# A Hyena and latent-attention encoder layer: the implicit filter on 128 rows of half the times, constant tables in two parts over GpSimd's queue

## Chip, cores and metric

The kernel runs on one core of a Trainium2 chip. The metric is the device time of one execution in microseconds (us); lower is better. The cores' engines are TensorE (PE, with its weight loads as PEld), VectorE (DVE), ScalarE (ACT), GpSimd (POOL) and SyncE (SP), which here only issues DMAs. Each engine works off its own list of instructions in order, and each DMA queue belongs to the engine that issues on it.

## The reference

One layer on x of 1024 x 1024 in float32: a root-mean-square norm, one input projection of 5,280 columns, a Hyena branch with two gated long convolutions, a branch of latent attention with eight heads, gates, and an output projection. The change touches the implicit filter of the long convolutions:

```python
def hyena_filter_spectra(L, w_f1, b_f1, freq_1, w_f2, b_f2, freq_2, w_f3):
    ...
    z = jnp.concatenate([t, jnp.cos(ang), -jnp.sin(ang)], axis=-1)
    h = jnp.sin(freq_1 * (z @ w_f1 + b_f1))
    h = jnp.sin(freq_2 * (h @ w_f2 + b_f2))
    k = (h @ w_f3).reshape(L, HY_ORDER, 2, HY_WIDTH)
    ...
    k = k * decay[:, None, None, :]
    k_full = jnp.concatenate([k[:, :, 0], k[::-1, :, 1]], axis=0)
    return jnp.fft.rfft(k_full.astype(jnp.float32), axis=0)
```

L is 1024, z has 33 columns, h has 64, HY_WIDTH is 512. The filter has two directions, and the second runs through time backwards.

## The kernel before, in words

Products of float32 are made from parts: a value is split into a high part (a cast to the PE's fp32r type, on ScalarE) and a low part (the difference, on VectorE), by `split` and `gsplit`. `mm3` makes a product from three matmuls: high by high, low by high, high by low. So each operand costs a ScalarE cast and a VectorE subtraction before TensorE can use it.

The work around the change comes in this order.

- `load_x` loads x as eight tiles of 128 x 1024, by SyncE's and ScalarE's queues in turn.
- `filter_loads` issues on SyncE's queue the constant selection matrix (`selr`), the two hidden weights, and the network's input table `z2` of 128 x 1024: rows 0 to 32 hold z, rows 64 to 96 hold z with reversed time. So the 128 rows carry both directions of the filter, and all 1024 times stand in the columns.
- `build_hT` makes the normalised, transposed x. It takes the sums of squares on both engines, then a reciprocal root of twelve small VectorE operations (`rsqrt`), scales x (`xs`, L223), transposes it on TensorE (`ptx`, L230), and splits what it gets from PSUM (`hh` on ScalarE, L142; `hl` on VectorE, L143). It does so for two halves of the times, of four x tiles each.
- `filter_mlp` is the two hidden layers. Each goes in two groups of 512 times: three matmuls into one PSUM bank (`pf`), then `sin_layer` with six VectorE steps over 128 x 512 (bias and frequency L254, turns L255 and L256, three reductions L258 and a clamp L260) and the sine on ScalarE (L261), whose table must be loaded when another function ran before (ACT_TABLE_LOAD). The first layer's output is split into `h1h` and `h1l`; of the second's, `h` holds for each direction the high part on its 64 rows, and the residual on the other 64 (L305, L306).
- `filter_tables` loads the last layer's weights by ScalarE's queue, puts their high part on both row halves with four casts of 64 x 1024 (`w3h`, L319), the low part on one and zeros on the other (`w3l`, L322), and splits the forward transform's table `ku` (`kuh`, `kul`).
- `filter_spectra` multiplies `h` by `w3h` and `w3l` (`pk`, L348 and L349, 128 x 256 each), applies the decay (`kk`), and transforms the filters (`forward`, `pu`).
- `fill_g` are blocks of the input projection (`proj_block`): 48 matmuls of 128 x 512 each (`pm`, L567) on weights of 128 x 4 x 128 (`wr`, L559, two buffers on SyncE's queue; `wh`, `wl` their parts, L138, L139). They need nothing of the filter. The scheduler of the tile framework sets them between the filter's instructions on TensorE, so that they fill its waits. It fixes each engine's order when the program is built. An eviction `ob` (L683) ends a block.
- `load_gu` loads and splits the tables of the later transforms (`gu`) while the convolutions are under way.

## Time and profile before

| | |
|---|---|
| runs, us | 1154.97, 1155.45, 1157.68; median 1155.45 |
| profiled execution | 1159.08 us, span 1156.9 us |
| mean granted TensorE clock | 0.984 of full speed |
| busy share of the span | PE 95%, PEld 79%, DVE 77%, ACT 51%, POOL 9% |
| chain that ended last | PE 77%, DVE 8%, DMA 8%, ACT 4%, issue 2%, POOL 1% |

The profile is of one execution. A busy time is the sum over an engine's instructions; the share is of the span. The chain that ended last is followed back from the last instruction, at each step to what released it. In the timelines a number in brackets is the engine's idle time ahead of the instruction, with what ended it. A matmul's time includes its way through the array, so matmuls overlap: what one costs in a row of many is the distance of their starts.

### The profile page before, as it was taken

The numbers are of one execution on the slowest core, as the hardware profiler recorded it, in microseconds if no ns is written. First come the engines' busy times: TensorE is split into PE (matmuls) and PEld (weight loads), VectorE is DVE, ScalarE is ACT, GpSimd is POOL, SyncE is SP. The second block draws the span as 40 slices with busy tenths as digits, with TensorE's granted clock in tenths as the row PEclk, the third lists the DMA queues.
The fourth block names the chain that finished last, engine by engine and source line by source line (L and its number), as shares of the span: only waits on it lengthen the run. The fifth ranks groups of instructions, "written<-read, shape, count | busy, mean of one in ns | idle before, by whom it ended". The sixth has DMA issues, their size and how long they took to land.

```text
span 1156.9 us, 15518 instructions
## 1 busy us (share of the span) xinstructions
PE 1098.8 (95%) x5525; PEld 912.7 (79%) x5525; DVE 894.0 (77%) x1631; ACT 589.2 (51%) x1097; POOL 106.7 (9%) x108
## 2 busy tenths in 40 slices
PE   4899999999999999999998999799999999999996
PEld 3678888888888888878887887688888888777875
DVE  6988788698788886778774793488888888678872
ACT  5735655754445434434424752687777777321420
POOL 0000000000000000000000132400000000232253
PEclk9989999999999999999999999899999999999999
DMA  5446454642335334334327558610202010886345
GB/s 211 132 146 194 153 166 175 204 119 64 88 90 142 110 110 131 91 90 125 91 82 226 153 152 284 201 56 12 90 1 92 1 65 1 265 272 208 90 129 182
DMA packets 119221, 150.27 MB, mean 130 GB/s; under 512 B 8548, under 2 KB 82408, under 8 KB 119144
## 3 DMA queue, kind: packets, MB, share of 16 engines
q1 hardware_dynamic: 107688, 120.97, 34.4%
q10 hardware_dynamic: 11456, 28.32, 6.5%
q8 instruction: 43, 0.70, 0.3%
q14 instruction: 34, 0.28, 0.1%
HBM read 101.81 MB, written 47.45 MB: 129 GB/s over the span
## 4 chain that ended last, share of the span: by engine, by line
PE 77%; DVE 8%; DMA 8%; ACT 4%; issue 2%; POOL 1%; SPq 0%; POOLq 0%; ACTq 0%; DVEq 0%
PE pm L567 35%; PE pu L128 8%; PE pt L901 5%; PE pi L128 4%; PE S L119 2%; PE S L121 2%; PE S L122 2%; PE pv L913 2%; PE pv L914 2%; PE po L122 2%; PE po L121 2%; PE po L119 2%; PE pmo L121 1%; PE pmo L119 1%; ACT pr L888 1%
## 5 line engine op out<-in xcount | busy, mean ns | idle before, releaser
L567 PE MATMUL pm<-hh,wh 128*128 128x512 f32 x656 | 208.8, 394 | 1.4 <-DVE hl L143 0.5
L567 PE MATMUL pm<-hl,wh 128*128 128x512 f32 x656 | 209.4, 394 | 0.0
L567 PE MATMUL pm<-hh,wl 128*128 128x512 f32 x656 | 208.3, 392 | 0.1
L567 PEld LDWEIGHTS pm<-hh,wh 128*128 128x128 f32 x656 | 123.1, 189 | 27.3 <-ACT wh L138 0.7
L567 PEld LDWEIGHTS pm<-hh,wl 128*128 128x128 f32 x656 | 123.4, 189 | 26.0 <-DVE wl L139 0.5
L567 PEld LDWEIGHTS pm<-hl,wh 128*128 128x128 f32 x656 | 123.5, 189 | 25.4
L138 ACT CAST wh<-wr 128x512 fp32r<-128x512 f32 x98 | 60.3, 621 | 152.0 <-PE pm L567 106.9
L138 ACT CAST PTh<-pt 128x512 fp32r<-128x512 f32 x128 | 72.8, 587 | 43.6 <-PE pt L901 41.8
L139 DVE TENSOR_TENSOR PTl<-pt,PTh 128x512 fp32r<-128x512 f32 x128 | 84.0, 683 | 14.0 <-ACT PTh L138 13.7
L886 DVE TENSOR_REDUCE mx<-S 128x1 f32<-128x1024 f32 x64 | 77.8, 1218 | 10.5 <-PE S L122 10.1
L139 DVE TENSOR_TENSOR wl<-wr,wh 128x512 fp32r<-128x512 f32 x95 | 66.2, 702 | 16.2 <-ACT wh L138 16.1
L901 PE MATMUL pt<-ident,pr 128*128 128x128 f32 x512 | 75.1, 276 | 1.1 <-ACT pr L888 0.2
L888 ACT ACTIVATE pr<-S,mx 128x1024 f32<-128x1024 f32 x64 | 71.7, 1121 | 5.4 <-DVE mx L886 5.1
L901 PEld LDWEIGHTS pt<-ident,pr 128*128 128x128 f32 x512 | 59.1, 140 | 15.5 <-ACT pr L888 2.9
L913 PE MATMUL pv<-PTh,vc 128*128 128x256 f32 x256 | 68.9, 297 | 0.0
L914 PE MATMUL pv<-PTl,vc 128*128 128x256 f32 x256 | 67.8, 293 | 0.0
L473 DVE TENSOR_TENSOR t<-pu,kt 128x512 f32<-128x512 f32 x64 | 41.0, 681 | 31.2 <-PE pu L128 30.5
L138 ACT CAST rh<-res 128x512 fp32r<-128x512 f32 x64 | 39.5, 619 | 42.8 <-PE pu L128 20.2
L119 PE MATMUL S<-kh,qh 96*128 96x512 f32 x128 | 53.0, 414 | 1.7 <-ACT pr L888 1.6
L121 PE MATMUL S<-kh,ql 96*128 96x512 f32 x128 | 52.5, 410 | 0.0
L913 PEld LDWEIGHTS pv<-PTh,vc 128*128 128x128 f32 x256 | 48.5, 189 | 4.4 <-DVE at L924 1.6
L122 PE MATMUL S<-kl,qh 96*128 96x512 f32 x128 | 50.8, 398 | 0.0
(285 smaller groups left out, 2402.2 us busy)
## 6 DMA issues: line engine op xcount, KB each, us to landing
wr<-in_w_in_dram SPq DMA_DIRECT2D x82, 256.0 KB, 3.2
wor<-in_w_out_dram SPq DMA_DIRECT2D x36, 256.0 KB, 4.6
dec<-in_dec_dram SPq DMA_DIRECT2D x16, 512.0 KB, 3.7
gT<-ob ACTq DMA_DIRECT2D x16, 512.0 KB, 3.3
gg<-gT SPq DMA_DIRECT2D x16, 512.0 KB, 3.9
kd<-kt ACTq DMA_DIRECT2D x28, 256.0 KB, 2.2
kt<-kd SPq DMA_DIRECT2D x28, 256.0 KB, 2.7
m<-gg ACTq DMA_DIRECT2D x16, 256.0 KB, 3.5
```

Source lines behind the costliest of these rows:

```text
L119: m = nc.tensor.matmul(out, lhsT=lh, rhs=rh, start=start, stop=False)
L121: nc.tensor.matmul(out, lhsT=ll, rhs=rh, start=False, stop=False)
L122: nc.tensor.matmul(out, lhsT=lh, rhs=rl, start=False, stop=stop)
L128: m = self.nc.tensor.matmul(out, lhsT=x, rhs=y, start=n == 0, stop=n == len(ops) - 1)
L138: self.behind(self.nc.scalar.copy(out=hi, in_=x), after)
L139: (eng or self.nc.vector).tensor_tensor(out=lo, in0=x, in1=hi.bitcast(F32), op=ALU.subtract)
L567: nc.tensor.matmul(ps[c][0:m], lhsT=w[:, i, 0:m], rhs=h[d][:, c * 512:(c + 1) * 512], start=(d == 0 and f == 0), stop=(d == 7 and f == 2))
L886: nc.vector.tensor_reduce(out=mx, in_=ps, axis=AX.X, op=ALU.max, negate=True)
L888: nc.scalar.activation(out=pr, in_=ps, func=AF.Exp, bias=mx, accum_out=RS[h // 2][:, qb, h % 2:h % 2 + 1])
L901: nc.tensor.transpose(out=pt[:, i], in_=pr[:, kb * P:(kb + 1) * P], identity=self.ident)
L913: nc.tensor.matmul(pv, lhsT=V[h][:, kb], rhs=hi[:, kb], start=(kb == 0), stop=False)
L914: nc.tensor.matmul(pv, lhsT=V[h][:, kb], rhs=lo[:, kb], start=False, stop=(kb == 7))
```

## The change

The input table holds half as many columns: rows 0 to 32 carry the first 512 times, rows 64 to 96 the last 512. Each hidden layer is then one group of three matmuls and one `sin_layer`. That has two reductions in place of three, and one buffer of each kind. The filter of reversed times is no longer computed: a VectorE copy reads `h` with reversed columns. Since both directions now need all 128 rows of the last layer's weights, these are loaded on both row halves by four loads on SyncE's queue, and split like any other operand, in 128 x 1024.

The tables `z2`, `ku` and `gu` are split on the host, and `sel` is passed as fp32r. GpSimd's queue loads all of them straight into their places: the first five behind a copy that waits for the seventh x tile, `guh` and `gul` later. The splits of these tables on ScalarE and VectorE go. Ahead of the real transposes stand 36 of raw x whose result nobody reads.

```diff
-    z2 = np.zeros((P, L), f32)
-    z2[:33] = z.T
-    z2[64:97] = z[::-1].T
+    z2 = np.zeros((P, L // 2), f32)
+    z2[:33] = z[:L // 2].T
+    z2[64:97] = z[L // 2:].T
...
+    for n, x in (("z2", z2), ("ku", ku), ("gu", gu)):
+        t[n + "h"], t[n + "l"] = _parts(x)
...
+        idle = self.pp.tile([P, 512], F32, tag="tp", bufs=2, name="idle")
+        for i in range(4):
+            for j in range(8 if i < 3 else 12):
+                nc.tensor.transpose(out=idle[:, :P], in_=xt[i][:, (j % 8) * P:(j % 8 + 1) * P], identity=self.ident)
...
-        for c in (6.28125, 0.0019350051879882812, 3.019915981956753e-07):
+        for c in (6.28125, 2 * math.pi - 6.28125):
...
-        self.selr = f1.tile([P, P], F32, tag="selr", name="selr")
-        nc.sync.dma_start(out=self.selr, in_=a["sel"])
...
-        self.z2 = f1.tile([P, L], F32, tag="z2", name="z2")
-        nc.sync.dma_start(out=self.z2, in_=a["z2"])
+        self.wf3 = [f1.tile([P, 2, HY], F32, tag=f"wf3{d}", name=f"wf3{d}") for d in range(2)]
+        w3v = a["w_f3"][0].rearrange("k (o d c) -> d k o c", o=2, d=2)
+        for d in range(2):
+            for s in range(2):
+                nc.sync.dma_start(out=self.wf3[d][64 * s:64 * s + 64], in_=w3v[d])
+
+        dum = f1.tile([1, 1], F32, tag="dum", name="xdum")
+        last = nc.gpsimd.tensor_copy(out=dum, in_=self.xt[6][0:1, 0:1])
...
+        for t, x in ((self.z2[0], "z2h"), (self.z2[1], "z2l"), (self.kuh, "kuh"), (self.kul, "kul"), (self.sel, "sel")):
+            i = nc.gpsimd.dma_start(out=t, in_=a[x])
+            self.behind(i, last)
+            last = i
...
+        ps = self.pp.tile([P, L // 2], F32, tag="cv", bufs=CVB, name=self.nm("pf"))
+        self.mm3(ps, w1h, w1l, zh, zl, True, True)
+        x = self.sin_layer(f1, ps, fv[:, 0:1], fv[:, 1:2], L // 2)
+        self.split(x, h1h, h1l)
+        for d in range(2):
+            self.split(self.wf3[d], self.w3h[d], self.w3l[d], after=self.half0)
+        ps = self.pp.tile([P, L // 2], F32, tag="cv", bufs=CVB, name=self.nm("pf"))
+        self.mm3(ps, w2h, w2l, h1h, h1l, True, True)
+        x = self.sin_layer(f1, ps, fv[:, 2:3], fv[:, 3:4], L // 2)
         for c in range(2):
...
+            a_, b_ = slice(64 * c, 64 * c + 64), slice(64 - 64 * c, 128 - 64 * c)
+            h, r = self.h2[0, c], self.h2[1, 1 - c]
+            nc.scalar.copy(out=h[a_], in_=x[a_])
+            nc.vector.tensor_tensor(out=h[b_], in0=x[a_], in1=h[a_].bitcast(F32), op=ALU.subtract)
+            nc.vector.tensor_copy(out=r, in_=h[:, ::-1].bitcast(F32))
...
-        for i in range(2):
-            r = self.uq.tile([P, 11, P], F32, tag="UY", bufs=2, name=self.nm("gur"))
-            nc.sync.dma_start(out=r, in_=self.a["gu"][:, 11 * i:11 * i + 11])
-            self.split(r, self.guh[:, 11 * i:11 * i + 11], self.gul[:, 11 * i:11 * i + 11])
+        for t, x in ((self.guh, "guh"), (self.gul, "gul")):
+            nc.gpsimd.dma_start(out=t, in_=self.a[x])
```

The change moves instructions at three places that matter below; each list is one engine's own order.

On TensorE, ahead of the first spectrum product `pk` (`pm` with number 1630 and 1631 is the projection block that fills the wait; all `pm` rows here are of that block). Before:

```order
L567 MATMUL pm_1630<-hl_154,wh_1664 128x512
L567 MATMUL pm_1631<-hl_154,wh_1664 128x512
L567 MATMUL pm_1630<-hh_146,wl_1665 128x512
L567 MATMUL pm_1631<-hh_146,wl_1665 128x512
L348 MATMUL pk_475<-w3h_340,h_344 128x256
L349 MATMUL pk_475<-w3l_342,h_344 128x256
L348 MATMUL pk_475<-w3h_340,h_344 128x256
L349 MATMUL pk_475<-w3l_342,h_344 128x256
L348 MATMUL pk_481<-w3h_341,h_345 128x256
```

Now (the block that 1630 and 1631 were has the numbers 1617 and 1618; 1683 and 1684 are the next block; h_397 is a reversed copy):

```order
L569 MATMUL pm_1683<-hh_158,wh_1717 128x512
L569 MATMUL pm_1684<-hh_158,wh_1717 128x512
L569 MATMUL pm_1683<-hl_166,wh_1717 128x512
L350 MATMUL pk_462<-w3h_391,h_395 128x256
L351 MATMUL pk_462<-w3l_393,h_395 128x256
L350 MATMUL pk_462<-w3h_391,h_395 128x256
L351 MATMUL pk_462<-w3l_393,h_395 128x256
L569 MATMUL pm_1684<-hl_166,wh_1717 128x512
L569 MATMUL pm_1683<-hh_158,wl_1718 128x512
L569 MATMUL pm_1684<-hh_158,wl_1718 128x512
L350 MATMUL pk_468<-w3h_392,h_397 128x256
```

Before, the first `pk` stood right behind the end of the block. Now 33 matmuls of the next block stand between that end and `pk`: 53 instructions lie from the second layer's first matmul (`pf_428`) to `pk`, of which the twentieth is the last of block 1617 and 1618. Between the first layer's matmuls and the second's lie 43, and three more `pm` stand between the first `pk` and that on the reversed copy.

On ScalarE, around the two sines (`sx`). Before:

```order
L683 ACTIVATE ob_1692<-pm_1630,cols 128x512
L261 ACT_TABLE_LOAD
L261 ACTIVATE sx_398<-sx_398 128x512
L261 ACTIVATE sx_416<-sx_416 128x512
L305 CAST h_344<-sx_398 64x512
L305 CAST h_345<-sx_398 64x512
L305 CAST h_344<-sx_416 64x512
L305 CAST h_345<-sx_416 64x512
L683 ACT_TABLE_LOAD
L683 ACTIVATE ob_1692<-pm_1631,cols 128x512
```

Now:

```order
L147 CAST wh_1687<-wr_1685 128x512
L271 ACT_TABLE_LOAD
L271 ACTIVATE sx_413<-sx_413 128x512
L147 CAST wh_1717<-wr_1715 128x512
L147 CAST h1h<-sx_413 128x512
L147 CAST wh_1753<-wr_1751 128x512
L147 CAST wh_1783<-wr_1781 128x512
L683 ACT_TABLE_LOAD
L683 ACTIVATE ob_1679<-pm_1617,cols 128x512
L271 ACT_TABLE_LOAD
L271 ACTIVATE sx_432<-sx_432 128x512
L683 ACT_TABLE_LOAD
```

Behind the last of these rows stand the second half's eviction, `ob_1679<-pm_1618`, and then the casts h_395 and h_396. The first layer's sine (`sx_413`) and the cast of its output (`h1h`) stand behind and between casts of projection weights, and the second's (`sx_432`) behind an eviction of the block, with a table load on either side.

On SyncE's queue, behind the last x load. Before:

```order
L267 DMA selr<-in_sel_dram 128x128
L269 DMA wf_133<-in_wf_dram 128x128
L271 DMA wf_135<-in_wf_dram 128x128
L273 DMA z_137<-in_z_dram 128x1024
L559 DMA wr_1566<-in_w_in_dram 128x4x128
L559 DMA wr_1596<-in_w_in_dram 128x4x128
```

Now:

```order
L277 DMA wf_131<-in_wf_dram 128x128
L279 DMA wf_133<-in_wf_dram 128x128
L285 DMA wf_135<-in_w_f_dram 64x2x512 x2
L285 DMA wf_136<-in_w_f_dram 64x2x512 x2
L561 DMA wr_1553<-in_w_in_dram 128x4x128
L561 DMA wr_1583<-in_w_in_dram 128x4x128
```

Four loads of the last layer's weights (`w_f`) have come ahead of the first projection weights, and the selection matrix and the input table have left.

## Rows read from the trace of the kernel before

**Rows 1.** The page's part 1: busy us of each engine, share of span, instructions.

```profile
PE 1098.8 (95%) x5525; PEld 912.7 (79%) x5525; DVE 894.0 (77%) x1631; ACT 589.2 (51%) x1097; POOL 106.7 (9%) x108
```

**Rows 2.** Waits of PE over the whole span: us in total, times, longest us.

```profile
PE pk L348 <- DVE h L306: 5.9, 1, 5.9
...
PE pq L119 <- ACT q L794: 1.8, 1, 1.8
```

**Rows 3.** Windows, columns: PE, PEld, DVE, ACT, POOL busy (x), PEclk, DMA share, GB/s.

```profile
60.00:65.00 5.00, 4.55 (x14) 3.58 (x14) 4.07 (x7) 2.18 (x4) 0.00 (x0) 0.50 0.55 170
```

**Rows 4.** Timeline of PE, 45 to 67 us: start, us, line, form, [idle before].

```profile
45.67 0.61 PE L567 MATMUL pm<-hl,wh 128*128 128x512 f32 x2
...
49.02 0.62 PE L567 MATMUL pm<-hh,wh 128*128 128x512 f32 x2
...
51.77 0.62 PE L567 MATMUL pm<-hh,wh 128*128 128x512 f32 x2
...
52.68 0.61 PE L567 MATMUL pm<-hh,wl 128*128 128x512 f32 x2
59.19 0.58 PE L348 MATMUL pk<-w3h,h 128*128 128x256 f32 x1 [5.90 <-DVE h L306]
...
66.07 0.63 PE L567 MATMUL pm<-hh,wl 128*128 128x512 f32 x2
```

**Rows 5.** Groups of DVE, 25 to 60 us: busy us, mean ns, idle before.

```profile
L258 DVE SCALAR_TENSOR_TENSOR sx<-sk,sx 128x512 f32<-128x512 f32 x12 | 7.6, 688 | 0.0
L254 DVE TENSOR_SCALAR sx<-pf,cols 128x512 f32<-128x512 f32 x4 | 3.1, 807 | 0.1
...
L322 DVE TENSOR_TENSOR w3l<-wf,w3h 64x1024 fp32r<-64x1024 f32 x2 | 2.4, 1218 | 0.0
...
L256 DVE TENSOR_SCALAR sk<-sk 128x512 f32<-128x512 f32 x4 | 1.6, 422 | 0.0
```

**Rows 6.** Groups of ACT, 25 to 70 us.

```profile
L319 ACT CAST w3h<-wf 64x1024 fp32r<-64x1024 f32 x4 | 4.2, 1049 | 3.1 <-DMA wf<-in_w_f_dram 3.0
L683 ACT ACT_TABLE_LOAD x3 | 3.8, 1283 | 0.1
...
L683 ACT ACTIVATE ob<-pm,cols 128x512 f32<-128x512 f32 x4 | 2.8, 688 | 1.9 <-PE pm L567 1.9
...
L138 ACT CAST zh<-z 128x512 fp32r<-128x512 f32 x2 | 1.1, 620 | 0.0
```

**Rows 7.** Weight loads: the page's part 6; then the first eight's landing alone.

```profile
wr<-in_w_in_dram SPq DMA_DIRECT2D x82, 256.0 KB, 3.2
...
DMA to landing us min/median/max: 3.0/4.3/5.1
```

**Rows 8.** Timeline of the start, 15 to 31 us.

```profile
15.95 6.01 PE L230 MATMUL ptx<-ident,xs 128*128 128x128 f32 x28 [8.63 <-DVE xs L223]
...
17.75 0.62 ACT L138 CAST wh<-wr 128x512 fp32r<-128x512 f32 x1 [0.18 <-DMA wr<-in_w_in_dram]
...
20.92 0.17 DVE L158 SCALAR_TENSOR_TENSOR ry<-rt,ry 128x4 f32<-128x4 f32 x1
...
22.47 0.50 PE L567 MATMUL pm<-hh,wh 128*128 128x512 f32 x1 [0.51 <-DVE hl L143]
...
22.80 0.40 PE L567 MATMUL pm<-hl,wh 128*128 128x512 f32 x1
...
28.98 1.47 PE L230 MATMUL ptx<-ident,xs 128*128 128x128 f32 x12
```

**Rows 9.** Windows of the start, columns as in rows 3.

```profile
5.00:10.00 5.00, 0.45 (x1) 0.18 (x1) 0.86 (x1) 2.43 (x3) 0.00 (x0) 1.00 1.03 417
```

**Rows 10.** A window where the gate tables are split, columns as in rows 3.

```profile
210.00:240.00 30.00, 29.84 (x147) 24.79 (x146) 19.99 (x31) 20.39 (x35) 0.26 (x4) 1.00 0.64 189
```

**Rows 11.** A window in the attention's projections, columns as in rows 3.

```profile
660.00:690.00 30.00, 28.24 (x133) 25.20 (x132) 29.07 (x99) 20.06 (x41) 10.47 (x9) 0.94 0.53 159
```

**Rows 12.** Timeline of DVE at the first filter layer.

```profile
36.57 0.81 DVE L254 TENSOR_SCALAR sx<-pf,cols 128x512 f32<-128x512 f32 x1
```

More of the change, by code (lines that the diff above doesn't have):

```diff
@@ L39, with _parts, near @@
     _r += _c
+def _parts(x):
+    def near(v):
+        u = np.ascontiguousarray(v, np.float32).view(np.uint32)
+        return ((u + 0x7FF + ((u >> 12) & 1)) & np.uint32(0xFFFFF000)).view(np.float32)
+    hi = near(x)
+    return hi, near(x - hi)
 def _constants():
@@ L187, in columns @@
         self.ssc = cp.tile([P, 2, 8], F32, tag="ssc", name="ssc")
-    def selection(self):
-        self.sel = self.cp.tile([P, P], F32R, tag="sel", name="sel")
-        self.nc.scalar.copy(out=self.sel, in_=self.selr)
     def load_x(self, xp, g):
@@ L250, in sin_layer @@
         n = cols
-        x = fp.tile([P, n], F32, tag="sx", bufs=2, name=self.nm("sx"))
-        k = fp.tile([P, n], F32, tag="sk", bufs=2, name=self.nm("sk"))
+        x = fp.tile([P, n], F32, tag="sx", name=self.nm("sx"))
+        k = fp.tile([P, n], F32, tag="sk", name=self.nm("sk"))
         mg = 12582912.0
@@ L298, in filter_mlp @@
-        for c in range(2):
-            sl = slice(c * 512, (c + 1) * 512)
-            ps = self.pp.tile([P, 512], F32, tag="cv", bufs=CVB, name=self.nm("pf"))
-            self.mm3(ps, w2h, w2l, h1h[:, sl], h1l[:, sl], True, True)
-            x = self.sin_layer(f1, ps, fv[:, 2:3], fv[:, 3:4], 512)
-            for d in range(2):
-                a_, b_ = slice(64 * d, 64 * d + 64), slice(64 - 64 * d, 128 - 64 * d)
-                nc.scalar.copy(out=self.h2[d][a_, sl], in_=x[a_])
-                nc.vector.tensor_tensor(out=self.h2[d][b_, sl], in0=x[a_], in1=self.h2[d][a_, sl].bitcast(F32), op=ALU.subtract)
@@ L308, in filter_tables @@
-    def filter_tables(self, fp):
-        nc, a = self.nc, self.a
-        self.kuh = fp.tile([P, 18, P], F32R, tag="kuh", name="kuh")
-        self.kul = fp.tile([P, 18, P], F32R, tag="kul", name="kul")
-        with self.pool("fp2") as f2:
-            wf3 = f2.tile([P, 2, HY], F32, tag="wf3", name="wf3")
-            w3v = a["w_f3"][0].rearrange("k (o d c) -> d k o c", o=2, d=2)
-            for d in range(2):
-                nc.scalar.dma_start(out=wf3[64 * d:64 * d + 64], in_=w3v[d])
-            for d in range(2):
-                for s in (slice(0, 64), slice(64, 128)):
-                    nc.scalar.copy(out=self.w3h[d][s], in_=wf3[64 * d:64 * d + 64])
-                s = slice(64 * d, 64 * d + 64)
-                nc.gpsimd.memset(self.w3l[d][64 - 64 * d:128 - 64 * d].bitcast(F32), 0.0)
-                nc.vector.tensor_tensor(out=self.w3l[d][s], in0=wf3[s], in1=self.w3h[d][s].bitcast(F32), op=ALU.subtract)
-            for i in range(2):
-                kur = f2.tile([P, 9, P], F32, tag="kur", bufs=2, name=self.nm("kur"))
-                nc.scalar.dma_start(out=kur, in_=a["ku"][:, 9 * i:9 * i + 9])
-                self.split(kur, self.kuh[:, 9 * i:9 * i + 9], self.kul[:, 9 * i:9 * i + 9])
@@ L346, in filter_spectra @@
                         for i in range(2):
-                            ts = slice((2 * tp + i) * P, (2 * tp + i + 1) * P)
-                            nc.tensor.matmul(ps[:, i], lhsT=h2[d][:, ts], rhs=w3h[d][:, o, cs], start=True, stop=False)
-                            nc.tensor.matmul(ps[:, i], lhsT=h2[d][:, ts], rhs=w3l[d][:, o, cs], start=False, stop=True)
+                            b = 2 * tp + i
+                            h = h2[d, b // 4][:, b % 4 * P:(b % 4 + 1) * P]
+                            nc.tensor.matmul(ps[:, i], lhsT=h, rhs=w3h[d][:, o, cs], start=True, stop=False)
+                            nc.tensor.matmul(ps[:, i], lhsT=h, rhs=w3l[d][:, o, cs], start=False, stop=True)
                         nc.vector.tensor_tensor(out=kk[:, d], in0=ps, in1=dec[:, d], op=ALU.mult)
@@ L1167, in hyena_mla_kernel @@
                     k.load_x(xp, 1)
-                    k.filter_loads(f1)
+                    k.filter_loads(fp, f1)
                     k.build_hT(hp, xp)
                     k.filter_mlp(fp, f1)
-                    k.selection()
                 svw = ExitStack()
                 k.vw = svw.enter_context(k.pool("vw", side="right"))
-                with k.pool("fpb") as fb:
-                    k.filter_tables(fb)
-                    with k.pool("fwk") as wk:
-                        k.filter_spectra(wk)
-                        for b in range(GEARLY):
-                            k.fill_g(b)
+                with k.pool("fwk") as wk:
+                    k.filter_spectra(wk)
+                    for b in range(GEARLY):
+                        k.fill_g(b)
             with k.pool("uq") as k.uq, k.pool("gp") as gp, k.pool("vb") as k.vb:
```

36 lines of the change are left out of this document (15 added, 21 removed).

## The prediction

> **What bounds the kernel now.** I read the shares first: TensorE is busy for 1098.8 us, 95% of the span [rows 1], so time is won only where it idles, runs slowly, or does something unneeded. The list of its waits names such places. One of the longest lies in the part that the change touches: 5.9 us for the filter's last residuals [rows 2]. The granted clock, by stretches, then shows that the wait costs more than its own length: the stretch behind it stands at 0.50, which is 1.2 of 2.4 GHz [rows 3].
>
> In TensorE's timeline around it two projection matmuls take about 0.456 us (51.77 to 52.68 holds four), or 0.228 each. A 128x256 matmul has half the columns; I price it at half, 0.114, an estimate. The last work before the wait starts at 52.68 and covers 0.46; matmuls run at full pitch again from 66.07. Those 12.93 us hold 8 short and 10 long matmuls, 0.91 + 2.28 = 3.19 us of full-speed work. So **9.7 us** are lost: 5.90 idle before the first spectrum product, the rest, 3.8, behind it, nearly all of it for the low clock [rows 4]. Similarly from 46.13 (45.67 plus two matmuls) to 49.02 there are 2.89 us for 8 matmuls, 1.82: another 1.1 lost, at the second layer.
>
> The reason is what runs elsewhere then: VectorE works off two half-groups of range reduction and the splits of constants, ScalarE the casts of four [rows 5, 6].
>
> **The change part by part.** The sum is made against the profiled execution (1159.08 us, span 1156.9) and then taken from the median of the runs, 1155.45, which is 3.6 us lower.
>
> *The filter in one group.* Six 128x512 matmuls go: 6 x 0.228 = **-1.4**. Half of the VectorE and ScalarE work goes too, but that was paid only through the two waits.
>
> *The wait before the spectra.* 33 projection matmuls of the next block now stand between the second layer and the first spectrum product, where before there was none of another block. I follow the new chain from the second layer's start, at 0. TensorE has 53 matmuls to issue: 53 x 0.228 = 12.1. ScalarE must first evict the previous projection block, whose last matmul is the twentieth: 4.6. Then come an eviction of 0.69, a table load of 1.28, the sine (0.62, like any 128x512 cast), a table load, an eviction and a cast: 4.6 + 0.69 + 1.28 + 0.62 + 1.28 + 0.69 + 0.62 = 9.8 [rows 5, 6]. The residual on VectorE is ready at 10.5, 1.6 before TensorE is there. The second filter's input needs one cast more, a second residual and two reversed copies. The trace has no reversed copy. Below, a plain 128x512 operation takes 0.42; above, I allow 1.4 (twice a two-input one); the nearest, and my value, is 0.69 [rows 5]. That gives 12.6, against TensorE at 12.1 + 4 x 0.114 + 3 x 0.228 = 13.2: a wait of 0 to 1. With the slack at 0.6 I put in half a us. The lost 9.7 go, 0.5 comes: **-9.7 + 0.5**.
>
> *The wait before the second layer.* Now 43 matmuls cover it, 9.8 us. But ScalarE's sine stands behind the cast of weights whose load is issued only after VectorE has read the buffer's last contents: 0.81 + 1.22 (w3l) + 0.42 + 0.69 = 3.14. The load takes 3.0 to 5.1 [rows 7]. Then cast, table, sine, cast and split of the layer's output: 0.62 + 1.28 + 0.62 + 0.62 + 0.62 = 3.8. The sum is 9.9 to 12.0, so the wait 0.1 to 2.2. The median of all these loads, 3.2, makes it 0.3, that of the first eight, 4.3, makes it 1.4. I take the middle: a lost 1.1 goes, 0.9 comes, **-1.1 + 0.9**.
>
> *The last-layer weights.* Two casts of 128x1024, 1.05 each, now stand where ScalarE cast the network's input (two of 0.62), in a stretch where it evicts transposes without a gap: 2.1 - 1.24 = **+0.9** [rows 6].
>
> *The start.* The idle transposes fill time in which TensorE waited (8.63 us). Twenty-eight real ones took 6.01, or 0.215 each, and later, in the flow, twelve took 1.47, or 0.12 [rows 8]. The idle ones cost nothing themselves: the last twelve need the fourth slice of x, 12 x 0.215 = 2.6 us, and behind the same slice VectorE still does a square, twelve small operations (0.17 each, 2.0) and a scaling before the real ones can start. Warm, the real ones would end by 19.3 instead of 21.96. But the first eviction's residual also waits for VectorE's chain of small operations, which ends at 20.92 + 0.17. The first projection matmul at 22.47 can thus come at most some 0.6 earlier. Against that, 0.46 MB more stand ahead of the first projection weights on SyncE's queue (four weight loads of 0.26 come, the input table's 0.52 and a small one of 0.07 go), 1.1 us at the 417 GB/s that the x loads reached [rows 9], and 2.95 MB of tables on GpSimd's queue (2 x 0.26, 2 x 1.18, 0.07) share the engines. If both queues got half, the second weights, cast at 17.75 before, would be there 1.1 + 0.96 / 0.417 = 3.4 us later, at 21.2. Cast and residual take 1.3: 22.5, where 22.47 less 0.6 is wanted. Bounds: -0.6, and +5 if the whole 3.4 MB go first (17.75 + 8.2 + 1.3 = 27.2). I take **+0.8**, near the half share.
>
> By the Trainium skill ("TensorE: Matmul & The Clock Gate", "Part 4: PE-mode transpose") transposes do not raise the clock. By that rule the idle ones would be useless, and the term would be some 0.6 worse. The trace speaks against it: after nothing but 28 transposes the second projection matmul took 0.40 [rows 8], and one at full pitch takes 0.62 - 0.228 = 0.39 [rows 4].
>
> *The rest.* The gate tables' splits, which go, lie between 210 and 240 us, where TensorE is busy for 29.84 of 30: it covers them [rows 10], so 0. A load of U on SyncE's queue now waits for the last filter product; 68 long matmuls lie between the two uses, 15.5 us, against 5.1 for the slowest load [rows 7]: 0. GpSimd's queue waits for TensorE's spectrum products before it issues the gate tables, and what stands behind the wait there are small fills of padding columns; the tables' first use comes some 200 TensorE instructions later, about 40 us: 0.
>
> Sum: -1.4 - 9.2 - 0.2 + 0.9 + 0.8 = **-9.1**, so 1155.45 - 9.1 = **1146.4** (profiled: 1150.0). The forecast's own range runs from 1142.7 (no new waits, casts hidden, start -0.6: -12.8) to 1149.5 (waits of 1.0 and 2.2, casts 1.0, start +2: -6.0).
>
> **The rivals.** *A: the sine is late again.* The weight load lands at 5.1 or the reversed copies cost 1.4, in one of the two places. A wait of 1.8 us lies in a stretch of clock 0.94 [rows 2, 11], so one of 2 to 3 us can bring back up to 3.4 us of low clock: 1146.4, plus 1 to 2.2 more of wait, plus 2.6 to 3.4, 1150 to 1152. For it: loads here vary from 3.0 to 5.1 [rows 7]. Against it: the wait must reach about 2 us at the second layer; my sum gives that only at the slow end. 0.13.
>
> *B: the first projection weights land behind GpSimd's tables.* The start costs 5, not 0.8: 1150.6. For it: 2.95 MB stand in a queue of their own. Against it: the weights keep a queue of their own, and 1.5 MB on it would have to wait for 2.95 on the other. 0.07.
>
> *C: A and B together, or the wait is only moved,* within 0.3% of before, 1152.0 to 1158.9. That is 3.5 us, about what a measurement tells from no change. 0.08.
>
> *D: slower.* The network's input now comes only over GpSimd's queue; no row of before has a load there, and all of TensorE stands behind the first layer in its order. VectorE takes its result at 36.57 [rows 12], so TensorE needs the table at about 36. If the loads land later, each us is lost in full. The gain is gone 9.1 later, from about 45; the kernel is slower by over 0.3% from about 49. Loads 20 us late would give 1166. Against it: x is all in when the second chain of small operations starts, before 20.92, and 0.52 MB need 1.3 us at 417 GB/s, the whole 2.95 need 7.1 [rows 9]. A cover of 15 us stands against 7. 0.07.
>
> The Trainium skill has a mechanism for D ("SBUF — State Buffer", "SBUF: two separate sides"): descriptors of GpSimd's queue cannot be written while VectorE runs certain two-port operations. VectorE is busy nearly all the time here; no run yet shows how much that holds up.
>
> **How the numbers follow.** Forecast 0.65, A 0.13, B 0.07, C 0.08, D 0.07. Faster by over 0.3%: 0.65 + 0.13 + 0.07 = 0.85; same 0.08; slower 0.07. The range reaches from 1142.2, the forecast's own low end less 0.5 for the runs' scatter (1154.97 against 1155.45), to 1152.0, the top of A and B; C and D are left out.
>
> **What would show it.** Right: the 5.90 wait before the spectra is gone or below 1, and the clock stays at 1.00 in the slices from 50 to 65 us; the first projection matmul stands between 21.9 and 23.3; GpSimd's first two loads land before 30. A shows as a wait of TensorE on ScalarE's split of the first layer's output, or on a copy, with a low clock behind it; B as a wait on the first weights near 22; D as a wait of TensorE or its weight load on the table at 36. Wrong altogether would be a span whose early part is shorter by 9 and whose end is not: then something later takes the time back, which the rows of before do not show.

## The result: one per cent slower, and the profile after

| | before | after |
|---|---|---|
| median of the runs, us | 1156.29 (4 runs) | 1167.88 (4 runs) |
| ratio to before, 95% interval | | 1.0097 (1.0078 to 1.0116) |
| profiled execution, us | 1159.08 | 1167.1 |
| span of it, us; mean granted clock | 1156.9; 0.984 | 1165.3; 0.982 |

The forecast was 1146.4 with a range from 1142.2 to 1152.0. The change is slower by 11.6 us between the medians, by 8.0 between the profiled executions. Three stretches account for most of it. These are windows (columns as in [rows 3]); first the kernel before, in stretches not shown ahead:

```profile
0.00:45.00 45.00, 28.51 (x143) 24.09 (x144) 33.49 (x75) 29.88 (x47) 2.09 (x6) 1.00 0.50 167
45.00:90.00 45.00, 38.18 (x172) 30.94 (x171) 40.19 (x73) 23.16 (x38) 0.00 (x0) 0.89 0.50 162
210.00:270.00 60.00, 59.32 (x285) 49.04 (x284) 43.09 (x74) 32.76 (x59) 0.53 (x8) 1.00 0.52 151
600.00:720.00 120.00, 114.27 (x530) 97.53 (x529) 81.65 (x241) 55.81 (x109) 19.52 (x16) 0.97 0.61 190
```

and the kernel after:

```profile
0.00:45.00 45.00, 23.07 (x126) 19.75 (x127) 22.77 (x56) 22.71 (x38) 3.55 (x10) 0.85 0.73 235
45.00:90.00 45.00, 44.59 (x216) 36.42 (x215) 35.13 (x61) 20.28 (x30) 0.00 (x0) 1.00 0.43 129
210.00:270.00 60.00, 53.59 (x244) 43.59 (x243) 40.93 (x76) 29.85 (x58) 1.59 (x10) 0.94 0.59 189
600.00:720.00 120.00, 116.25 (x551) 97.98 (x550) 89.21 (x255) 58.51 (x114) 19.25 (x16) 1.00 0.56 172
```

Read busy time times clock as full-speed work. From 45 to 90 us TensorE does 44.6 instead of 38.18 x 0.89 = 34.0: the 10.6 us that the filter's waits cost are won. From 210 to 270 it does 53.59 x 0.94 = 50.4 instead of 59.3: 8.9 lost, where I had put 0. In the first 45 us it falls far behind, although 36 idle transposes are in its count. Measured where VectorE takes the first layer's result, at 47.75 instead of 36.57 [rows 12], the start costs 11.2; I had put 0.8. With the 1.4 us of removed matmuls: 11.2 - 10.6 + 8.9 - 1.4 = 8.1, against the 8.0 measured. That it fits so well is in part chance. The sum leaves out the stretch from 600 to 720 us, where the change does 116.3 us of full-speed work instead of 114.27 x 0.97 = 110.8, and the stage behind it, where it loses some of that again (720 to 750: 18.70 x 0.89 = 16.6 instead of 21.11 x 0.89 = 18.8). The second loss comes out smaller in the time of the runs below that take it away.

**The start.** The chain that ended last, after, from 14 to 37 us (start, us, what):

```profile
14.42 13.69 DMA wr<-in_w_in_dram
28.13 0.63 ACT wh L147
28.79 0.69 DVE wl L148
29.59 0.17 DVE rt L166
29.95 0.67 DVE hl L152
30.66 5.47 PE pm L569 x13
```

The first weights are cast at 27.25, before at 16.94. Their load takes 13.7 us, where the slowest of the first eight took 5.1 before [rows 7]. The timeline (after) shows both ends, and further down the filter and the second loss:

```profile
15.64 3.28 PE L240 MATMUL ptx<-ident,xs 128*128 128x128 f32 x28 [2.26 <-DVE xs L233]
27.25 0.62 ACT L147 CAST wh<-wr 128x512 fp32r<-128x512 f32 x1 [11.13 <-DMA wr<-in_w_in_dram]
30.66 0.80 PE L569 MATMUL pm<-hh,wh 128*128 128x512 f32 x1 [11.75 <-DVE hl L152]
31.25 0.63 PE L569 MATMUL pm<-hl,wh 128*128 128x512 f32 x1
31.68 0.63 PE L569 MATMUL pm<-hh,wl 128*128 128x512 f32 x1
...
57.82 0.50 PE L128 MATMUL pf<-h1h,w2h 128*128 128x512 f32 x1 [0.34 <-ACT h1h L147]
...
70.21 0.39 PE L350 MATMUL pk<-w3h,h 128*128 128x256 f32 x1
...
238.01 1.94 PE L613 MATMUL ptt<-ident,acc 128*128 128x128 f32 x8 [5.00 <-DVE acc L602]
```

TensorE names VectorE's `hl`, but VectorE itself stood behind `wl`, which needs the cast of the late weights. The first projection matmul stands at 30.66 instead of 22.47 [rows 8], and then the pitch is 0.43 (31.25 to 31.68): the granted clock is 0.50 from 30 to 35 us and 0.95 in the next five. The real transposes, behind the idle ones, took 3.28 us for 28, about half of the 6.01 before [rows 8]: that part works, and TensorE then idles 11.75. The wait of 5.90 ahead of the spectra [rows 2, 4] is gone: no idle time stands before the first `pk`. The second layer's wait is 0.34.

Why the weights are late, the DMA issues of 10 to 15 us (after; size, median us to landing) begin to say:

```profile
kuh<-in_kuh_dram POOLq DMA_DIRECT2D x1, 1152.0 KB, 10.3
kul<-in_kul_dram POOLq DMA_DIRECT2D x1, 1152.0 KB, 12.7
wf<-in_w_f_dram SPq DMA_DIRECT2D x3, 256.0 KB, 6.4
wr<-in_w_in_dram SPq DMA_DIRECT2D x2, 256.0 KB, 14.1
```

and the queues within 19.5 to 23.5 us (packets, MB, share of 16 engines), where q0 is GpSimd's and q1 SyncE's:

```profile
q0 software_dynamic: 264, 1.47, 95.1%
q1 hardware_dynamic: 260, 0.13, 18.6%
```

Both queues get as many packets through, 264 and 260, but GpSimd's carries eleven times the bytes: a row of `kuh` goes as long packets, one of projection weights in runs of 512 bytes. Engines that serve the two queues in turns, packet by packet, would do just this. The Trainium skill says it ("DMA: Bandwidth & Descriptors", "Queues, rings and completion order": each engine goes round the queues that have work, a packet at a time); the two counts agree. The weights also stand behind 1 MB of last-layer weights on their own queue, and these move slowly: 0.45 MB from 14 to 16 us, when nothing else was loaded, or 225 GB/s, where x came at 417 [rows 9].

**The second loss.** The output tables, 1.4 MB each, are issued by GpSimd's queue at 217.42 and 217.94 and land after 8.1 and 12.4 us. Beside them the short blocks' loads (`kd`) land after 8.2 (217 to 235 us), before after 2.7 (205 to 235). ScalarE stands still for one of them (after):

```profile
229.90 0.60 ACT L369 ACTIVATE kt<-pu 128x512 f32<-128x512 f32 x1 [6.56 <-DMA kd<-kt]
```

`acc` begins on ScalarE, behind it, and ends on VectorE. So it is late, and TensorE waits 5.00 at 238.01, with a granted clock of 0.63 from 240 to 245. From 224 to 227 us three queues were busy, GpSimd's, ScalarE's with `kd` (q10) and SyncE's:

```profile
q0 software_dynamic: 87, 0.92, 83.9%
q10 hardware_dynamic: 80, 0.16, 14.3%
q1 hardware_dynamic: 85, 0.04, 7.6%
```

Again nearly as many packets each, and very different bytes.

### The profile page after: what moved, and what is told of

Read it like the earlier page. It is cut to its first block, busy times and chain, and to the rows that moved or that the text cites. A ratio compares the mean times of both kernels' runs of the same rounds, so it can differ in the third digit from the quotient of the medians.

```text
span 1165.3 us, 15570 instructions
## 1 busy us (share of the span) xinstructions
PE 1101.0 (94%) x5555; PEld 912.5 (78%) x5555; DVE 879.1 (75%) x1608; ACT 578.6 (50%) x1083; POOL 109.5 (9%) x114
## 4 chain that ended last, share of the span: by engine, by line
PE 61%; DMA 15%; DVE 13%; ACT 5%; issue 3%; POOL 1%; SPq 0%; POOLq 0%; DVEq 0%; ACTq 0%
PE pm L569 29%; PE pu L137 7%; PE pt L901 5%; PE pi L137 4%; DMA wr<-in_w_in_dram 3%; DMA wor<-in_w_out_dram 2%; PE S L128 2%; PE S L130 2%; PE S L131 2%; PE pv L913 2%; PE pv L914 2%; ACT pr L888 1%; DMA m<-gg 1%; DMA x<-in_x_dram 1%; DMA yr<-yT 1%
## 5 line engine op out<-in xcount | busy, mean ns | idle before, releaser
L569 PE MATMUL pm<-hl,wh 128*128 128x512 f32 x656 | 212.4, 395 | 0.0
L569 PEld LDWEIGHTS pm<-hh,wh 128*128 128x128 f32 x656 | 123.7, 189 | 40.5 <-DVE hl L152 12.0
L148 DVE TENSOR_TENSOR PTl<-pt,PTh 128x512 fp32r<-128x512 f32 x128 | 84.0, 682 | 13.9 <-ACT PTh L147 13.7
L886 DVE TENSOR_REDUCE mx<-S 128x1 f32<-128x1024 f32 x64 | 77.8, 1217 | 10.5 <-PE S L131 10.3
```

The lines of the kernel that those rows point to most:

```text
L148: (eng or self.nc.vector).tensor_tensor(out=lo, in0=x, in1=hi.bitcast(F32), op=ALU.subtract)
L569: nc.tensor.matmul(ps[c][0:m], lhsT=w[:, i, 0:m], rhs=h[d][:, c * 512:(c + 1) * 512], start=(d == 0 and f == 0), stop=(d == 7 and f == 2))
L886: nc.vector.tensor_reduce(out=mx, in_=ps, axis=AX.X, op=ALU.max, negate=True)
```

## The experiments

Three theories stood at first. T1: turns by packet, so that the tables' long rows crowd out the weights. T2: only the volume counts. T3: GpSimd's queue itself holds the others up, the more so the more runs it has to describe. Later the question became which load does it: the input tables (`ku`), or the last-layer weights (`w_f`) ahead of the projection weights. The runs' own "before" had medians of 1155.4 to 1157.9; the ratios below are to it. Every kernel computes the whole layer.

**e1: the tables `ku` in 512-byte runs,** at the same place of the same queue.

```diff
-            i = nc.gpsimd.dma_start(out=t, in_=a[x])
+            for n in range(2 if x[:2] == "ku" else 1):
+                q = slice(9 * n, 9 * n + 9)
...
+                    i = nc.gpsimd.dma_start(out=t[:, q], in_=a[x][q].rearrange("i p c -> p i c"))
```

> The forward tables kuh and kul are loaded at the same moment on GpSimd's queue, the same bytes, but in runs of 512 B (stored the other way round in memory, four loads in place of two) instead of runs of 9,216 B. Theory T1, the DMA engines serve the queues packet by packet, so that long packets take nearly all bytes: the first projection weights are cast at 19 to 23 us instead of 27.25, the first projection matmul starts at 24 to 27 instead of 30.66, the time falls by 3 to 8 us to 1160 to 1165. Rival T2, only the volume counts: cast at 27 or later, 1167 to 1170. Rival T3, the software queue itself holds the others up through its descriptors: four times as many descriptors, cast later than 27.

Measured: 1166.83, ratio 1.0092 (1.0073 to 1.0111). The first weights are cast at 23.72 instead of 27.25, the first projection matmul comes at 28.13. That is T1's direction, a little outside its ranges for the start and 1.8 us above the one for the time; T2 and T3 had the cast at 27 or later. But the bytes were not loaded at the same moment: GpSimd's queue issued the first of the four loads at 13.86 and the others only at 26.19, 32.64 and 37.63. By the cast a quarter of the bytes was under way, so the 3.5 us do not tell length from volume. The pace does, while both queues were busy, from 22 to 23 us (e1):

```profile
q0 software_dynamic: 274, 0.14, 70.2%
q1 hardware_dynamic: 273, 0.14, 69.5%
```

The counts are equal again, and now the bytes are too: the weights got 0.14 MB in this one us, in the change 0.13 in four. These are turns by packet, as T1 has them. But 6.8 of the 10.3 us remain, and the total hardly moves.

**e2: `ku` only behind the second sine.**

```diff
-        for t, x in ((self.z2[0], "z2h"), (self.z2[1], "z2l"), (self.kuh, "kuh"), (self.kul, "kul"), (self.sel, "sel")):
+        for t, x in ((self.z2[0], "z2h"), (self.z2[1], "z2l"), (self.sel, "sel")):
...
         x = self.sin_layer(f1, ps, fv[:, 2:3], fv[:, 3:4], L // 2)
+        last = nc.gpsimd.tensor_copy(out=f1.tile([1, 1], F32, tag="dum2", name="xdum2"), in_=x[0:1, 0:1])
+        for t, n in ((self.kuh, "kuh"), (self.kul, "kul")):
+            i = nc.gpsimd.dma_start(out=t, in_=self.a[n])
```

> kuh and kul alone are moved: their loads wait for the second layer's sine, some 15 us before their first use; the input table and sel stay. T1 and T2: the first weights are cast at 18 to 20, the first projection matmul starts at 21.9 to 24, and the time falls by 8 to 11 us to 1157 to 1160; the 5.00 us wait of the transposes of acc near 238 stays, earlier by as much. Rival: the late start is due to the four loads of w_f ahead of the weights or to the idle transposes; then the first matmul stays beyond 27 and the time above 1164. Second rival: the burst only moves, and the weights of the blocks at 55 to 75 come late; then a wait of 3 us or more stands there.

Measured: 1165.13, ratio 1.0078 (1.0058 to 1.0098); first cast 23.34, first matmul 26.74. The forecast is missed by 5 us. With no long table in the stretch the weights are still 6.4 us later than before. So `ku` explains 3.9 of the 10.3 us, and something else the rest.

**e3: the output tables issued earlier,** ahead of the third short block's fills.

```diff
...
+                if hf == 0 and b == 1:
+                    self.load_gu(self.gp)
...
-                k.load_gu(gp)
```

> Only guh and gul are moved: on GpSimd's queue they now stand ahead of the small fills of the third short block instead of behind them, so that they are issued as soon as the last spectrum product is done (near 195 instead of 217.4), when little else loads. T1 and T2: the 5.00 us wait at 238 and the low clock behind it go, the time falls by 6 to 10 us to 1158 to 1162. Rival: that wait comes from the order of the short convolution on VectorE and ScalarE, not from the loads; then it stays and the time is 1166 to 1169.

Measured: 1165.40, ratio 1.0081 (1.0061 to 1.0101). The longest wait of the output transposes is 1.8 instead of 5.0, and the clock stays at 1.00 from 210 to 270, nearly as forecast; the time is only 2.5 us below the change, where 6 to 10 were forecast. In this execution the start was some 1.7 us later (first matmul 32.32). The first product on `guh` comes at 240.44 all the same, in the change at 246.39. Behind 600 us the lead is given back: from 630 to 660 the granted clock is 0.94 here and 1.00 in the change. Why was not tried.

**e4: e2 and e3 together.**

> Both moves together. If the two bursts are all that separates the change from the forecast, the two gains add: 14 to 20 us below the change, 1147 to 1154, which is faster than the kernel before by 2 to 9 us. Rival: the filter's gain of 9 to 10 us was never there or is given back later; then 1155 to 1158, the same as before.

Measured: 1159.09, ratio 1.0022 (1.0008 to 1.0036): 8.8 us below the change, where 14 to 20 were forecast, and still 0.2% above before. Against e2 the output tables' move is worth 6.0 us here (1165.13 to 1159.09), and the first product on `guh` comes 7.5 us earlier (235.46 against 242.94). The first cast stays at 23.26. From 14 to 19 us the engines moved 219 GB/s, where x came at 417 [rows 9], most of it last-layer weights and network input.

**e5: e4, and the last-layer weights over GpSimd's queue behind the first half of the normalised input.**

```diff
-        for d in range(2):
-            for s in range(2):
-                nc.sync.dma_start(out=self.wf3[d][64 * s:64 * s + 64], in_=w3v[d])
...
+        last = nc.gpsimd.tensor_copy(out=f1.tile([1, 1], F32, tag="dum3", name="xdum3"), in_=self.hl[0][0:1, 0:1].bitcast(F32))
+        for d in range(2):
+            for s in range(2):
+                i = nc.gpsimd.dma_start(out=self.wf3[d][64 * s:64 * s + 64], in_=self.w3v[d])
```

> As e4, and the four loads of the last layer's weights (w_f, 1.05 MB in rows of 2 KB) no longer stand ahead of the first projection weights on SyncE's queue; they go by GpSimd's queue, behind the first half's first low part, and their casts stand behind the second half's evictions. Theory: these loads are what still holds the first projection weights up in e4 (cast at 23.3 there, 16.94 before); the cast then comes at 17 to 19.5, the first projection matmul at 21.9 to 23.7, and the time falls by 3 to 6 us to 1153 to 1156. Rival: the input table's two loads on GpSimd's queue do it; then the cast stays beyond 21 and the time above 1157.

Measured: 1154.08, ratio 0.9983 (0.9971 to 0.9996). The first weights are cast at 15.95. But in this program's order their `wl` stands ahead of x's scaling on VectorE, which waits 2.45 for that cast: the real transposes start at 20.07 behind 4.21 of idle time, at a granted clock of 0.50, and the first matmul is still at 26.59.

**e6: e5 without the idle transposes.**

> As e5 without the 36 idle transposes. The prediction's reading: they shorten the real transposes from 6.0 to 3.3 us, but the first low part waits for VectorE's chain or for the weights anyway; so 0 to +0.8 us against e5. Rival (the clock falls in the gap that is left behind the short transposes): without them the real ones end later, the gap is shorter, the clock stays up, and the time is 0.5 to 2 us below e5. Second rival: they warm the clock for good, and it is 2 to 4 us slower without them.

Measured: 1152.81, ratio 0.9976 (0.9966 to 0.9985). The 28 transposes take 5.50 us from 19.98, the first matmul is at 26.40. Nothing is lost without the idle ones; the time is in the range of the first rival.

**e7: the network alone:** half the times, last-layer weights on both halves, but `z2`, `ku`, `gu` and `sel` loaded and split as before, and no idle transposes.

```diff
-    z2 = np.zeros((P, L), f32)
+    z2 = np.zeros((P, L // 2), f32)
...
+        self.split(self.z2, zh, zl, after=self.half0)
...
             for d in range(2):
-                nc.scalar.dma_start(out=wf3[64 * d:64 * d + 64], in_=w3v[d])
+                for s in range(2):
+                    nc.scalar.dma_start(out=wf3[d][64 * s:64 * s + 64], in_=w3v[d])
```

> The half-times network alone on top of the kernel before: one group per layer, two reductions, the reversed copies, weights on both row halves; the tables are loaded by the queues of before in float32 and split on ScalarE and VectorE as before, and there are no idle transposes. On TensorE only 18 long matmuls lie between the second layer and the first spectrum product here, where the change has 50. Theory, that a half of the filter's gain comes from those 33 matmuls and the rest from the shorter chain: the start is as before (first matmul near 22.5), a wait of 3 to 6 us before the spectrum products stays, with a low clock behind it, and the time is 1151 to 1154. Rival: the shorter chain alone ends the wait, and the time is 1146 to 1149. Second rival: the network brings nothing, 1155 to 1158.

Measured: 1157.35, ratio 1.0020 (1.0008 to 1.0032). The forecast was 1151 to 1154; the second rival's range holds it. The smaller network alone wins nothing in this run, and the waits of TensorE from 10 to 90 us say why:

```profile
PE ptx L239 <- DVE xs L232: 11.3, 1, 11.3
PE pk L354 <- DVE h L313: 5.7, 1, 5.7
```

The wait ahead of the spectra is back at 5.7: with `ku` split on both engines in that stretch, only 21 matmuls stood between the second layer's first one and the first `pk`, 53 in the change. The start is late too, by the order of e5: VectorE waits 2.02 for the first weights' cast ahead of x's scaling, and the first projection matmul is at 24.39 instead of 22.47. So the network is worth more than this run shows, by up to 1.9 us. The gain needs the network and the host's split of `ku` (e11); the split without the network was not tried.

**e8: e7 with the idle transposes.**

> As e7 with the 36 idle transposes. With the first weights on time, the real transposes end some 2.7 us earlier, and the first projection matmul then waits for VectorE's chain of small operations, which ends near 21.1: it starts 0.3 to 0.8 earlier than in e7, and the time is 0 to 1 us below it. Rival: the gap between the real transposes and the first projection matmul grows to 3 us, the clock falls, and the time is 0.5 to 3 us above e7.

Measured: 1161.15, ratio 1.0047 (1.0034 to 1.0060): 3.8 us worse than e7. That is beyond the rival's 3. Behind a gap of 4.59 the real transposes still took 4.94, and the granted clock was 0.77 from 20 to 25 us. But the loss does not lie there: the first projection matmul starts at 24.24, in e7 at 24.39, and the first product on `guh` at 236.94, in e7 at 237.46. What e8 loses it loses later, and the cause stays open.

**e9: e6 with the first weights' casts behind the first scaling of x;** **e10: the same with the idle transposes;** **e11: e7 with that order, and the `ku` parts over GpSimd's queue behind the second sine.**

```diff
-                nc.vector.tensor_scalar(out=x, in0=xt[4 * g + i], scalar1=rs[:, i:i + 1], scalar2=None, op0=ALU.mult)
+                xi = nc.vector.tensor_scalar(out=x, in0=xt[4 * g + i], scalar1=rs[:, i:i + 1], scalar2=None, op0=ALU.mult)
...
+            self.xs0 = getattr(self, "xs0", xi)
...
-            self.split(raw[:, :, 0:m], wh[:, :, 0:m], wl[:, :, 0:m])
+            self.split(raw[:, :, 0:m], wh[:, :, 0:m], wl[:, :, 0:m], after=self.xs0)
```

> As e6 (no idle transposes, w_f, ku and gu loads moved), and the casts of the first projection weights stand behind the scaling of x, as they did in the kernel before: in e6 VectorE waits 2.46 us for such weights ahead of the scaling, and the real transposes start at 19.98 instead of 15.95. Theory: the scaling comes at 15.2 again, the first projection matmul at 22 to 23, and the time falls by 2 to 4 us to 1149 to 1151. Rival: the DMA-bound stage near 720 takes it back, 1152 to 1154.

> As e9 with the 36 idle transposes: what they are worth when the weights are on time. e8 against e7 and e5 against e6 showed a loss of 3.8 and 1.3 us, with a low clock after a gap of 4.2 to 4.6 us between idle and real transposes. Theory, the loss came from that gap (the idle ones end at 13.4, the real ones started at 18 to 20): with the real ones at 15.9 the gap is 2.3 to 2.6 us, the clock stays up, the real transposes take 3.3 us, and the first projection matmul comes 0.3 to 0.8 earlier than in e9: -1 to 0 us. Rival: the gap behind the real transposes, about 2.5 us, brings the low clock: +1 to +3 us.

> As e7 (tables split on the chip as before, no idle transposes), but kuh and kul come in parts over GpSimd's queue behind the second sine, so that ScalarE and VectorE no longer split ku between the two layers and the spectra; casts of the first weights behind the scaling of x as in e9. Theory: it is these splits that held the spectra back in e7; without them 50 instead of 21 matmuls stand ahead of the first spectrum product, the wait of 5.72 us there goes, and the time is 1147 to 1151. Rival: the wait stays above 3 us, 1153 to 1157.

Measured: e9 1149.31, ratio 0.9936 (0.9920 to 0.9951); e10 1150.73, 0.9942 (0.9923 to 0.9961); e11 **1148.51, 0.9919 (0.9900 to 0.9939)**, the lowest median of all, in an interval that overlaps with e9's. e9 and e11 lie in the ranges of their forecasts; e10 was forecast 0 to 1 us below e9, and its median is 1.4 above. Of e11's gain over e7 (1.0%) a part is the order of the casts, which is worth 0.4% between e6 and e9. Waits of TensorE from 10 to 90 us in e11:

```profile
PE ptx L239 <- DVE xs L231: 8.7, 1, 8.7
PE pm L574 <- DVE hl L151: 2.6, 1, 2.6
PE pk L355 <- DVE kk L357: 0.5, 1, 0.5
PE pm L574 <- ACT hh L150: 0.5, 1, 0.5
```

and the windows of e11, where the clock stays at 1.00 in the stretch that had 0.50 in [rows 3]:

```profile
15.00:30.00 15.00, 11.92 (x67) 10.47 (x68) 13.39 (x31) 13.12 (x25) 0.00 (x0) 1.00 0.20 52
30.00:75.00 45.00, 44.07 (x220) 36.77 (x219) 36.34 (x59) 22.96 (x33) 1.37 (x3) 1.00 0.69 222
```

No wait for the filter's residual is left, and TensorE is busy for 44.07 of 45. From the second layer's first matmul 50 stand ahead of the first `pk`. e11 takes from the change only the network and the split `ku`; its `z2`, `sel` and `gu` are as before, and the last-layer weights come over ScalarE's queue. e9 and e10 have overlapping intervals: the idle transposes are worth nothing that shows, although the real ones behind them took 3.28 against 5.47.

**e12: the change without the idle transposes.**

> The change without its idle transposes, all else as it is. The first weights still land near 27, so the real transposes have time: 0 to -1 us against the change (a shorter gap ahead of the first projection matmul, the clock falls all the same): 1166 to 1168. Rival: the idle transposes are the cause of the late start; then 1157 to 1160.

Measured: 1165.76, ratio 1.0080 (1.0062 to 1.0099); first cast 27.61, first matmul 31.00 behind 10.22 of idle time. The idle transposes are not the cause of the late start.

**e13: the output tables in 512-byte runs,** at the same place.

```diff
-            nc.gpsimd.dma_start(out=t, in_=self.a[x])
+            for n in range(2):
+                q = slice(11 * n, 11 * n + 11)
+                nc.gpsimd.dma_start(out=t[:, q], in_=self.a[x][q].rearrange("i p c -> p i c"))
```

> The changed kernel with one difference: the tables of the output network are stored so that a partition's row comes in runs of 512 bytes instead of 11 KB, in two loads each, at the same place of GpSimd's queue. If the packets' length lets them crowd out their neighbours (turns by packet): the short blocks' loads land within 5 us (8.2 in the changed kernel), the wait of the first output transpose on the accumulator falls from 5.0 us to 2.5 or less, and the total falls by 3 to 6 us, to 1162 to 1165. If it is the volume alone: the wait stays at 4 to 6 us and the total at 1166 to 1169. The start is as in the changed kernel in either case (first weight cast near 27 us).

Measured: 1174.1, ratio 1.0139 (1.0108 to 1.0169): slower, against the forecast, though both its steps came true. The DMA issues of 217 to 235 us and the timeline of TensorE and GpSimd (e13):

```profile
kd<-kt ACTq DMA_DIRECT2D x5, 256.0 KB, 3.2
```

```profile
219.14 1.08 POOL L624 DMA_DIRECT2D guh<-in_guh_dram  x1 [0.48 <-issue]
225.81 1.07 POOL L624 DMA_DIRECT2D guh<-in_guh_dram  x1 [5.58 <-issue]
231.99 1.06 POOL L624 DMA_DIRECT2D gul<-in_gul_dram  x1 [5.11 <-issue]
...
243.16 1.07 POOL L624 DMA_DIRECT2D gul<-in_gul_dram  x1 [10.11 <-DVE w L383]
...
234.35 1.06 PE L613 MATMUL ptt<-ident,acc 128*128 128x128 f32 x8 [0.72 <-DVE acc L602]
...
244.32 0.58 PE L137 MATMUL pu<-rh,guh 128*128 128x256 f32 x1 [4.13 <-ACT rh L147]
248.87 0.58 PE L137 MATMUL pu<-rh,gul 128*128 128x256 f32 x1 [3.97 <-DMA gul<-in_gul_dram]
```

The neighbours are free again: `kd` lands after 3.2 instead of 8.2, the transposes' wait is 0.72 instead of 5.00. Shorter packets and fewer bytes beside them both have a part in that, and this run does not part them: GpSimd's queue moved 1.57 MB from 217 to 235 us, in the change 2.88. It now issues a table only after the one before it is nearly through, 5 to 6 us each; the last load lies behind another wait of GpSimd's and lands when TensorE has stood still for it. The tables were kept from their neighbours at the price of being late themselves. The start was also 1.5 us later in this execution (first matmul 32.13).

**e14: the change with the last-layer weights alone moved,** as in e5, with the order of e9; the `ku` tables stay in the burst.

> The changed kernel with one difference in what is loaded when: the last-layer weights' four loads go over GpSimd's queue behind the first half of the normalized input instead of over SP's queue at the start (and the first projection weights' casts are placed behind the first scaling of x, which took a scheduler's side effect of that move away in an earlier run). The input tables stay in the burst. If the input tables' long packets are the main cause: the first weight cast comes at 21 to 25 us instead of 27.3, the first projection matmul at 24 to 28, and the total is 1161 to 1166. If the last-layer weights are the main cause: the cast comes before 19 us, the matmul before 23, and the total is 1157 to 1161. The 5.0 us wait near 238 us stays by both.

Measured: 1156.66, ratio 0.9994 (0.9980 to 1.0009): 11.2 us below the change by the move of 1 MB (with the order that keeps the first weights' `wl` behind x's scaling), just below what was forecast for the last-layer weights as the main cause. Its timeline and the landing of `kuh`:

```profile
16.27 1.12 ACT L147 CAST wh<-wr 128x512 fp32r<-128x512 f32 x2
...
21.78 0.50 PE L575 MATMUL pm<-hh,wh 128*128 128x512 f32 x1 [2.59 <-DVE hl L152]
```

```profile
kuh<-in_kuh_dram POOLq DMA_DIRECT2D x1, 1152.0 KB, 6.3
```

The first projection weights are issued at 9.25 instead of 13.12, and the first two loads are in by 16.3 us, when the tables' packets have only begun; both casts are done at 17.39, where before the second began at 17.75 [rows 8]. The tables land sooner too, 6.3 us instead of 10.3. The later weights, caught in the burst, land after about 6 us, and TensorE has no wait for them. The wait near 238 is there as in the change, 4.88 at 226.52. With both tables' bursts moved as well (e10) the time is 5.9 us lower.

## Why the prediction was wrong

- **"The start", +0.8: this step failed; it measured 11.2.** The step let the two queues share the engines half and half by bytes and moved all bytes at 417 GB/s. Shared are packets, not bytes (264 and 260 packets, 1.47 and 0.13 MB). And the 1 MB of last-layer weights, taken as 0.46 MB net or 1.1 us, held the projection weights back until the burst had begun. They move at 225 GB/s, not at 417. With `w_f` ahead and no long tables the first cast is 6.4 us late (e2); with the tables and no `w_f` ahead it is not late at all, 16.27 (e14); with both, 10.3. The order on SyncE's queue is the main cause, the tables' packets make it worse. The upper bound of 5 was too low by the same two assumptions. (By the half share the step's own working gave 22.5, the start of before; the 0.8 was put on top.)
- **"The rest", 0 for the output tables: failed; it measured 8.9 in the windows, and 2.5 (e3) and 6.0 (e4 against e2) in the time of the runs that take the wait away.** The step looked at who waits for the tables and what stands behind them on GpSimd's queue. It did not ask who else uses the engines in those 12 us: the short blocks' loads (8.2 instead of 2.7). e3 takes the wait away by the moment; e13 does it with short runs, at a slower pace.
- **The waits, -9.7 + 0.5 and -1.1 + 0.9: right.** 10.6 won in the stretch, no wait before `pk`, 0.34 before the second layer, clock 1.00 from 45 to 90 us. What the prediction did not see is that it takes both parts: the network alone leaves 5.7 (e7).
- **The casts of last-layer weights, +0.9,** and the fewer matmuls, -1.4, cannot be told from the rest in these runs.
- **The idle transposes, 0: right in that they gain nothing.** They speed the real ones (3.28 against 5.5 for 28), but in all four pairs the kernel with them has the higher median, by 1.3 to 3.8 us (e5 and e6, e8 and e7, e10 and e9, the change and e12), in e8 beyond the intervals. The Trainium skill's rule ("TensorE: Matmul & The Clock Gate", "Part 4: PE-mode transpose"), by which transposes do not raise the clock, is not what the trace of e5 shows: the granted clock is 0.50 from 19 to 25 us and 1.00 from 26, and from 20.07 to its rise TensorE did nothing but the 28 real transposes. After a gap of 4.59 (e8) the clock was low again in spite of the idle ones.
- **The rivals.** B named half of the mechanism, the first weights behind GpSimd's tables, with 5 us as its price and 0.07 as its chance; the argument against it, that the weights keep a queue of their own, was the error, for on that queue they stood behind `w_f`. D, the only slower case, put the loss on the network's input, for which TensorE never waited. That two bursts could each cost about as much as the whole gain stood nowhere.

With both losses taken out and the order of the casts kept, a gain of the forecast's size is there: e9 stands 0.64% and e11 0.81% below before, where the prediction had 9.1 of 1155.45, 0.79%. That the size is right is in part luck: the prediction had no term for the stretch behind 600 us. There the 492 matmuls from the last `pty` to the last projection matmul take 113.2 us before, 108.6 in the change and 109.0 in e9, and why was not tried.

## What to carry to other kernels

Before a load is put on another queue, list what else is in flight in that stretch, and put the loads on each queue in the order of their first use: 1 MB that was needed some 20 us later, because it was issued first, held the first weights up by 6 us alone and cost 11 us beside the tables' burst. A table in long rows takes far more than its share from neighbours with short ones, so give it a moment when nobody waits; cutting it up instead can make it late itself (e13).

## What the runs showed of the hardware

- Equal turns by packet between a GpSimd queue and a SyncE queue: 264 to 260 packets, 1.47 to 0.13 MB in 4 us; with 512-byte runs on both, 274 to 273 packets, 0.14 MB each in 1 us (e1); with ScalarE's queue as a third, 87, 85 and 80 in 3 us.
- GpSimd's queue took a load of 1,408 packets (704 KB in runs of 512 bytes) only 5.1 to 5.6 us after the one before it (e13), loads of 1,152 such runs 4.0 to 11.3 us after (e1); two loads of 1,408 KB in long rows were issued 0.5 us apart.
- The last-layer weights, which fill 64 partitions at a time, moved slowly wherever they were: before, from 34 to 38 us, 0.37 MB in 40.5% of 16 engines' time, or 14 GB/s for each engine; x, on 128 partitions, 0.88 MB in 43.2% of 5 us, or 25. That the partitions are the reason was not tried; their runs are also 2 KB against 4 KB.
- The Trainium skill's mechanism for rival D ("SBUF — State Buffer", "SBUF: two separate sides"), descriptors of GpSimd's queue held up by VectorE, did not decide the start: TensorE waited for none of its tables. Whether it has a part in the long gaps between issues in e1 and e13 was not tried.
